# Strassen block products for four of eleven inner pairs of the second feed-forward matrix

## The chip, the cores and the metric

The kernel runs on one core of a Trainium2 chip. The metric is device time in microseconds (us), lower is better. One launch computes the whole two-layer trunk.

## The reference

A trunk of DEPTH = 2 layers over x of 256 tokens by 1024 channels, everything float32. Each layer has two feed-forward steps with a mixer between them. The change touches the feed-forward steps alone:

```python
def _swiglu(x, w1, w3, w2):
    return (jax.nn.silu(x @ w1) * (x @ w3)) @ w2
...
for l in range(DEPTH):
    h = _swiglu(x, ffn_w1[l, 0], ffn_w3[l, 0], ffn_w2[l, 0])
    x = _layernorm(ALPHA * x + 0.5 * h, ln_g[l, 0], ln_b[l, 0])
    h = _mixer(x, ...)
    x = _layernorm(ALPHA * x + h, ln_g[l, 1], ln_b[l, 1])
    h = _swiglu(x, ffn_w1[l, 1], ffn_w3[l, 1], ffn_w2[l, 1])
    x = _layernorm(ALPHA * x + 0.5 * h, ln_g[l, 2], ln_b[l, 2])
```

w1 and w3 are 1024 x 2816, w2 is 2816 x 1024. So there are four feed-forward steps in a launch, each with one product h @ w2 of 256 x 2816 by 2816 x 1024.

## The kernel before

**Precision.** A float32 operand is cut in two parts of a shorter format (F32R): `hi` is a ScalarE copy of the value, `lo` is a VectorE subtraction of `hi` from it. A product is then three matmuls, hi*hi, hi*lo and lo*hi (`three`, L205 to L208), all added up in one PSUM bank. A weight therefore needs one ScalarE and one VectorE instruction for each 128 x 1024 piece before the TensorE can read it.

**Streaming.** `stream` (L147) loads one chunk of 128 x 2048 float32 (1 MB) into a raw buffer, of which there are RAW = 4, and cuts it in pieces of 128 x 1024 (L166 for hi, L168 for lo). The pieces go to two pools, each with HL = 8 buffers (L42, L59, L60). A buffer comes free when the last matmul that reads it is done.

**The first half of a feed-forward step.** `gemm_a2` (L210) computes w1 and w3 products for two k tiles of h at a time, with h transposed, channels on the partitions: 32 matmuls of 512 columns with hi weights (L220) and 32 of 256 columns with lo weights (L227), then emptying of the banks (L228, L230), the silu, the multiplication (L524) and the split of h into `hh` and `hl` (L525, L174). It does so nine times. The first four k tiles of h come by another way (`gemm_first` or `gemm_b2`, and transposes).

**The second half, which the change rewrites.** h has 22 k tiles of 128 channels (FT = 22); w2 has two column halves of 512. `gemm_b` (L249) is called once for each half (L529, L536). In it, each k tile and each of the two token tiles of 128 costs one block product of 128 x 128 by 128 x 512, so three matmuls of 512 columns. The last `tail` k tiles are held, and done first for token tile 0, then for token tile 1, so that the norm of token tile 0 starts while token tile 1 is still on the TensorE. In the last feed-forward step of the launch, token tile 1 of the second half is computed as two blocks of 256 columns (`last`), so that only a quarter row is left for the end.

**The norm.** `Norm.part` (L412) adds a finished block to the scaled residual and takes statistics (L415, L419, in the last step also a multiplication, L421); `Norm.finish` (L423) normalizes a token tile; its transposes are put between later matmuls by counting beats.

**Order.** The TensorE's instructions run in the order in which the program writes them. The other engines' order is planned at build time: a scheduler takes, for each engine, the ready instruction of the lowest priority number, and the number grows by 1000 with each chunk (`step`, L105). On the chip each engine then runs its own list in order. PSUM has eight banks, four called main and four called side.

Of the kernel before, what the change touches and what calls it, by code (L numbers as in the profile page):

```python
# [11 lines left out]
F32 = mybir.dt.float32  # L12
F32R = mybir.dt.float32r
# [6 lines left out]
P = 128  # L20
# [5 lines left out]
DFF = 2816  # L26
FT = DFF // P
FB = 4
HEADS = 8
HD = 64  # L30
GROUPS = 8
# [16 lines left out]


@with_exitstack  # L50
def trunk(ctx, tc, x, xT, w13a, w13b, w2, wb, wqk, wa, wbr, wo, gateb, sgug, sgub, sguwT, sgubias, lam, diffg,
          lng, lnb, lngT, lnbT, cosT, sinT, out):
    nc = tc.nc
    V, A, G, PE = nc.vector, nc.scalar, nc.gpsimd, nc.tensor
# [15 lines left out]
    def name(s):  # L70
        serial[0] += 1
        return f"{s}_{serial[0]}"
# [11 lines left out]
    def view(tiles, per=2):  # L84
        return lambda k: tiles[k // per][:, (k % per) * T : (k % per + 1) * T]
# [57 lines left out]
    def behind(ins):  # L143

        return tc.issue_after(ins) if ins is not None else nullcontext()
# [93 lines left out]
    def rows_b(ps, t, k0, piece, xh, xl, kts, c0=0, n=512):  # L239
# [6 lines left out]
                  k == 0, k == kts - 1)  # L246
        beat(n / 1024)

    def gemm_b(src, kts, xh, xl, done, tail=4, last=()):  # L249

        blocks = [[(bank(), c, n) for c, n in (last if t else ()) or ((0, 512),)] for t in range(NT)]
        held = []
        for c in range(0, kts, 4):
            nk = min(4, kts - c)
            for i, piece in enumerate(stream(src[:, c * 512 : (c + nk) * 512], nk * 512)):
                k = c + 2 * i
                if k >= kts - tail:
                    held.append((k, piece))
                    continue
                for t in range(NT):  # L260
                    for ps, o, n in blocks[t]:
                        rows_b(ps, t, k, piece, xh, xl, kts, o, n)
        for t in range(NT):
            for ps, o, n in blocks[t]:
                for k, piece in held:
                    rows_b(ps, t, k, piece, xh, xl, kts, o, n)
                done(t, ps[:, :n], o, n)

    def gemm_b2(srcs, xh, xl, done, norm=None):

# [115 lines left out]
    class Norm:  # L386
# [25 lines left out]
        def part(self, t, c, ps):  # L412
            s = slice(c, c + ps.shape[1])
            with behind(self.xlo.get((0, 0))):
                V.scalar_tensor_tensor(out=self.y[t][:, s], in0=self.y[t][:, s], scalar=self.scale, in1=ps,  # L415
                                       op0=ALU.mult, op1=ALU.add)
            for o in range(s.start, s.stop, self.group):
                g = o // self.group * 6
                V.bn_stats(out=self.st[t][:, g : g + 6], in_=self.y[t][:, o : o + self.group])  # L419
            if self.last and t == NT - 1 and s.stop < D:  # L420
                V.tensor_tensor(out=self.y[t][:, s], in0=self.y[t][:, s], in1=self.g[:, s], op=ALU.mult)  # L421
# [70 lines left out]

    def ffn(l, f, i, norm, last=False):
        xh, xl = parts(both)
        h_hi = [act.tile([P, 512], F32R, tag="slot", name=name("hhi")) for _ in range(FT // 2)]
        h_lo = [act.tile([P, 512], F32R, tag="slot", name=name("hlo")) for _ in range(FT // 2)]
        hh, hl = view(h_hi), view(h_lo)

        def front(t, ps):
            s = t512("silu")  # L500
            A.activation(s, ps[0], AF.Silu)
            V.tensor_tensor(out=s, in0=s, in1=ps[1], op=ALU.mult)
            beside(turned(t, s), 2)

        def turned(t, s):
            b = side_bank()
            for k in range(FB):
                PE.transpose(b[:, k * P : (k + 1) * P], s[:, k * P : (k + 1) * P], ident)  # L508
            b4 = b.rearrange("p (k t) -> p k t", k=4)
            for j in range(2):  # L510
                hi = h_hi[j].rearrange("p (k t) -> p k t", k=2)[:, :, t * P : (t + 1) * P]
                lo = h_lo[j].rearrange("p (k t) -> p k t", k=2)[:, :, t * P : (t + 1) * P]
                split(hi, lo, b4[:, 2 * j : 2 * j + 2])
            yield 0

        if norm is None:
            gemm_first([w13b[l, f, 0], w13b[l, f, 1]], front)
        else:
            gemm_b2([w13b[l, f, 0], w13b[l, f, 1]], xh, xl, front, norm=norm)
        for j in range(FB, FT, 2):  # L520
            for m, z in gemm_a2([w13a[l, f, j - FB + m] for m in range(2)], both, lambda m: t512("silu")):
                s = z[:, :T]
                silu[0] = A.activation(s, s, AF.Silu).ins
                V.tensor_tensor(out=s, in0=s, in1=z[:, T:], op=ALU.mult)  # L524
# [6 lines left out]
        def done(t, p, c, n):  # L531
            ln.part(t, 512 + c, p)
            if c + n == 512:
                ln.finish(t, ((2, 1.5), (2, 1))[t])

        gemm_b(w2[l, f, 1], FT, hh, hl, done, tail=14, last=((0, 256), (256, 256)) if last else ())  # L536
        return ln.close()

    def mixer(l, i, norm):
# [222 lines left out]
    for l in range(DEPTH):  # L762
# [2 lines left out]
        norm = ffn(l, 1, 2, norm, last=l == DEPTH - 1)  # L765


_INS = ["x", "xT", "w13a", "w13b", "w2", "wb", "wqk", "wa", "wbr", "wo", "gateb", "sgug", "sgub", "sguwT", "sgubias",
        "lam", "diffg", "lng", "lnb", "lngT", "lnbT", "cosT", "sinT"]


def _layout(i):
    c = np.ascontiguousarray
    L = DEPTH
    f = {k: np.asarray(v) for k, v in i.items()}
    x = f["x"].reshape(T, D)
    o = {"x": x, "xT": c(x.reshape(T, KT, P).transpose(2, 1, 0)).reshape(P, KT * T)}

    def cols(w):

        k, n = w.shape[-2:]
# [24 lines left out]
    o["w13b"] = c(np.concatenate([halves(w1[..., :nb]), halves(w3[..., :nb])], axis=2))  # L806
    o["w2"] = halves(f["ffn_w2"])
# [40 lines left out]
```

## Time and profile before

| what | value |
|---|---|
| median of 3 runs | 1243.45 us (1243.18 to 1244.18) |
| span of the profiled execution | 1242.5 us, 0.95 us less than the median |
| TensorE matmul busy | 1236.6 us, 6703 instructions |
| VectorE busy | 873.1 us, 1532 instructions |
| ScalarE busy | 756.0 us, 1388 instructions |
| DMA | 241.87 MB, mean 195 GB/s |

The span is the time from the first to the last instruction of one profiled execution; the 0.95 us beside the median are what lies around it and the spread of runs. Busy time of an engine is the time in which at least one of its instructions ran. Matmuls overlap their neighbours, so what one costs is read from the distance of their starts, not from their length. In the rows "L208" is line 208 of the kernel, "bank<-whi,hhi" the output and the inputs by the program's names, "128x512" partitions by elements.

### The profile page before, as it was taken

How to read it: one execution, taken by the hardware profiler on the slowest of the kernel's cores; microseconds unless marked ns; L12 is line 12 of the kernel's file. 1: busy time of each engine (PE TensorE's matmuls, PEld its weight loads, DVE VectorE, ACT ScalarE, POOL GpSimd, SP SyncE). 2: the span in 40 equal slices, each digit the busy share in tenths (PEclk: the TensorE clock that was granted, in tenths of full speed). 3: DMA queues.
4: the chain of work that ended last, by engine and by line, in shares of the span. 5: the costliest groups of instructions: out<-in, count | busy, mean ns of one | idle time of the engine just before them, and what ended most of it. 6: DMA issues, size and time to landing. Idle time of an engine off the chain costs nothing.

```text
span 1242.5 us, 17870 instructions
## 1 busy us (share of the span) xinstructions
PE 1236.6 (100%) x6703; PEld 1064.1 (86%) x6703; DVE 873.1 (70%) x1532; ACT 756.0 (61%) x1388; POOL 86.0 (7%) x184
## 2 busy tenths in 40 slices
PE   9999999999999999999999999999999999999998
PEld 8888888888888888888888888888888888888887
DVE  6766567876587977665677665679756879766753
ACT  6776446679665566664466664466786555766640
POOL 0100000144100000000000000002430000000000
PEclk9999999999999999999999999999999999999999
DMA  9765645654754745556545546556556456455540
GB/s 352 276 204 183 224 171 187 227 167 165 248 183 145 244 162 205 177 180 253 194 169 191 192 159 250 203 184 206 162 175 228 165 174 233 170 203 203 165 174 35
DMA packets 40679, 241.87 MB, mean 195 GB/s; under 512 B 5344, under 2 KB 6416, under 8 KB 14480
## 3 DMA queue, kind: packets, MB, share of 16 engines
q1 hardware_dynamic: 36624, 227.82, 52.1%
q0 software_dynamic: 3536, 12.13, 3.0%
q8 instruction: 52, 0.85, 0.3%
q10 hardware_dynamic: 432, 0.79, 0.2%
q14 instruction: 35, 0.29, 0.1%
HBM read 235.47 MB, written 1.05 MB: 190 GB/s over the span
## 4 chain that ended last, share of the span: by engine, by line
PE 99%; DVE 0%; ACT 0%; issue 0%; DVEq 0%; ACTq 0%
PE bank L220 38%; PE bank L208 35%; PE bank L227 20%; PE bank L323 2%; PE sbank L588 1%; PE sbank L474 1%; PE sbank L637 1%; PE sbank L718 1%; PE sbank L335 0%; PE sbank L635 0%; PE sbank L659 0%; PE sbank L508 0%; PE sbank L622 0%; PE sbank L627 0%; PE sbank L446 0%; DVE xtok L454 0%
## 5 line engine op out<-in xcount | busy, mean ns | idle before, releaser
L168 DVE TENSOR_TENSOR wlo<-raw,whi 128x1024 fp32r<-128x1024 f32 (+1 forms) x442 | 490.0, 1127 | 223.4 <-PE bank L227 129.3
L166 ACT ACTIVATE whi<-raw 128x1024 fp32r<-128x1024 f32 (+1 forms) x442 | 425.8, 978 | 279.4 <-PE bank L208 135.3
L220 PE MATMUL bank<-x,whi 128*128 128x512 f32 x1792 | 426.5, 392 | 0.0
L220 PEld LDWEIGHTS bank<-x,whi 128*128 128x128 f32 x1792 | 330.7, 188 | 69.0 <-issue 2.6
L227 PE MATMUL bank<-x,wlo 128*128 128x256 f32 x1792 | 229.9, 284 | 0.0
L227 PEld LDWEIGHTS bank<-x,wlo 128*128 128x128 f32 x1792 | 224.2, 191 | 4.8
L208 PE MATMUL bank<-whi,hhi 128*128 128x512 f32 (+1 forms) x374 | 141.3, 378 | 0.0
L208 PE MATMUL bank<-wlo,hhi 128*128 128x512 f32 (+1 forms) x374 | 141.0, 377 | 0.0
L208 PE MATMUL bank<-whi,hlo 128*128 128x512 f32 (+1 forms) x374 | 140.9, 377 | 0.0
L228 ACT ACTIVATE r<-bank 128x256 f32<-128x256 f32 x256 | 96.5, 380 | 66.0 <-PE bank L227 65.7
L208 PE MATMUL bank<-whi,x 128*128 128x512 f32 x328 | 106.6, 394 | 0.0
L208 PEld LDWEIGHTS bank<-whi,hlo 128*128 128x128 f32 x374 | 70.4, 188 | 13.0
L208 PEld LDWEIGHTS bank<-wlo,hhi 128*128 128x128 f32 x374 | 70.4, 188 | 12.7
L208 PEld LDWEIGHTS bank<-whi,hhi 128*128 128x128 f32 x374 | 70.4, 188 | 12.7
L208 PEld LDWEIGHTS bank<-whi,x 128*128 128x128 f32 x328 | 61.6, 188 | 12.7
L208 PE MATMUL bank<-wlo,x 128*128 128x512 f32 x164 | 64.0, 390 | 0.0
L480 ACT ACTIVATE xf<-sbank,ln_b,ln_g 128x128 f32<-128x128 f32 x80 | 30.0, 456 | 40.2 <-PE sbank L474 40.2
L230 DVE TENSOR_TENSOR silu<-bank,r 128x256 f32<-128x256 f32 x144 | 54.2, 418 | 0.2
L383 POOL DMA_DIRECT2D bc<-in_lng x6 | 3.2, 530 | 727.7 <-DVE bc L382 727.7
L415 DVE SCALAR_TENSOR_TENSOR xtok<-xtok,bank 128x512 f32<-128x512 f32 (+1 forms) x25 | 16.6, 663 | 42.2 <-PE bank L208 42.2
L564 POOL TENSOR_TENSOR swap<-swap,sin_t 128x512 f32<-128x512 f32 x16 | 24.3, 1517 | 242.4 <-DMA swap<-z 226.7
L208 PE MATMUL bank<-lhi,x 128*128 128x512 f32 x120 | 39.9, 396 | 0.0
(183 smaller groups left out, 1254.1 us busy)
## 6 DMA issues: line engine op xcount, KB each, us to landing
raw<-in_w13a SPq DMA_DIRECT2D x72, 1024.0 KB, 5.0
raw<-in_w SPq DMA_DIRECT2D x40, 1024.0 KB, 4.9
raw<-in_wa SPq DMA_DIRECT2D x24, 1024.0 KB, 5.5
raw<-in_wb SPq DMA_DIRECT2D x16, 1024.0 KB, 4.9
raw<-in_wqk SPq DMA_DIRECT2D x16, 1024.0 KB, 5.1
raw<-in_wbr SPq DMA_DIRECT2D x16, 1024.0 KB, 4.9
raw<-in_w13b SPq DMA_DIRECT2D x12, 1024.0 KB, 5.0
raw<-in_wo SPq DMA_DIRECT2D x8, 1024.0 KB, 4.9
```

Source lines behind the costliest of these rows:

```text
L166: A.activation(h, r, AF.Copy)
L168: V.tensor_tensor(out=w, in0=r, in1=h.bitcast(F32), op=ALU.subtract)
L208: PE.matmul(ps, xx, w, start=start and n == 0, stop=stop and n == 2)
L220: PE.matmul(b[-1], hi[:, k * P : (k + 1) * P], xc(k), start=k == 0, stop=False)
L227: PE.matmul(b[n][:, :T], lo[:, k * P : (k + 1) * P], xc(k)[:, :T], start=False, stop=k == KT - 1)
L228: emptied[0] = A.activation(r[:, s], b[n][:, T:], AF.Copy, scale=scale).ins
L230: a = V.tensor_tensor(out=z[:, s], in0=b[n][:, :T], in1=r[:, s], op=ALU.add)
L323: PE.matmul(ps[t][m], x[:, j, o + t * P : o + (t + 1) * P], y, start=k0 + j == 0 and o == 0 and y is hi, stop=k0 + j == KT - 1 and y is lo)
L415: V.scalar_tensor_tensor(out=self.y[t][:, s], in0=self.y[t][:, s], scalar=self.scale, in1=ps, op0=ALU.mult, op1=ALU.add)
L474: PE.transpose(b[:, k * P : (k + 1) * P], self.y[t][:, h * 512 + k * P : h * 512 + (k + 1) * P], ident)
L480: A.activation(xf[:, s], b[:, s], AF.Identity, scale=self.gT[:, f], bias=self.bT[:, f])
L564: turned_by[0] = G.tensor_tensor(out=s3, in0=s3, in1=s, op=ALU.mult).ins
```

## The change

Of the eleven pairs of k tiles of h, four (k tiles 4 to 11) go through Strassen's scheme for 2 x 2 blocks: the two token tiles by the two k tiles of h, times the two k tiles by the two column halves of w2. Seven block products stand in place of eight. The other seven pairs stay as they were, and both column halves are now done together. The order on the TensorE is S, P, S, P, S, P, S (S a Strassen pair, P a plain pair), then the last four plain pairs, held, block by block: token tile 0 with both halves, then token tile 1 with both.

```diff
+NS = 4
+SQ = [(FB + 2 * p, FB + 2 * p + 1) for p in range(NS)]
+PQ = [(k, k + 1) for k in (0, 2, *range(FB + 2 * NS, FT, 2))]
...
-    act = ctx.enter_context(tc.tile_pool(name="act", bufs=27))
+    act = ctx.enter_context(tc.tile_pool(name="act", bufs=31))
...
+    def stream_s(src, pair):
...
+        a = (*pair, 0) if pair else None
+        if a is None:
+            pair = two()
+            a, keep = (*pair, 0), pair
+        else:
+            a, keep = (*pair, 512), None
+        b, c, d = ((*two(), 0) for _ in range(3))
+        cut(a, 0, 512)
+        cut(b, 1024, 1024)
+        V.tensor_tensor(out=raw[:, :1024], in0=raw[:, :1024], in1=raw[:, 512:1536], op=ALU.add)
+        cut(c, 0, 1024)
+        V.tensor_tensor(out=raw[:, 1024:1536], in0=raw[:, :512], in1=raw[:, 1024:1536], op=ALU.add)
+        V.tensor_tensor(out=raw[:, 1536:], in0=raw[:, 1024:1536], in1=raw[:, 1536:], op=ALU.add)
+        cut(d, 1024, 1024)
...
+        return keep, {1: at(a, 0), 3: at(b, 0), 2: at(b, 1), 5: at(c, 0), 7: at(c, 1), 6: at(d, 0), 4: at(d, 1)}
...
+        def mixed(q, qa):
+            qb = s512("qb")
...
+            for j, v in enumerate((qa, qb)):
+                split(at[0][j], at[1][j], v)
...
-                V.tensor_tensor(out=s, in0=s, in1=z[:, T:], op=ALU.mult)
-                split(hh(j + m), hl(j + m), s)
+                if (j, j + 1) in SQ:
+                    if m == 0:
+                        qa = s512("qa")
+                    V.tensor_tensor(out=qa[:, m * T : (m + 1) * T], in0=s, in1=z[:, T:], op=ALU.mult)
+                    if m:
+                        mixed((j, j + 1), qa)
...
-        gemm_b(w2[l, f, 0], FT, hh, hl, lambda t, p, c, n: ln.part(t, 0, p))
...
+        for n, q in enumerate(SQ):
+            pair, w = stream_s(w2s[l, f, n], pair)
+            for b in (3, 7, 4, 1, 2, 5, 6):
+                three(S[b], *s_op[q][b], *w[b], n == 0, n == NS - 1 and b in (1, 5, 6, 7))
+            beat(1.75)
+            if n < NS - 1:
+                plain_pair(False)
+        u, v = s512("u"), s512("v")
+        A.activation(u, S[6], AF.Copy)
+        ln.more(1, 0, S[7], ALU.subtract, ln.scale)
+        ln.more(0, 0, S[1], ALU.add, ln.scale)
+        V.tensor_tensor(out=u, in0=u, in1=S[1], op=ALU.add)
+        V.tensor_tensor(out=v, in0=S[5], in1=u, op=ALU.subtract)
+        ln.more(0, 1, v, ALU.add, ln.scale)
+        ln.more(1, 1, v, ALU.add, ln.scale)
+        ln.more(1, 0, u, ALU.add)
+        ln.more(1, 1, S[7], ALU.add)
+        while plain:
+            plain_pair(True)
+        for t in range(NT):
+            for c in range(2):
+                for ps, o, n in ends[t, c]:
+                    for q, w in held:
+                        rows_p(ps, t, q, w[c], hh, hl, o, n, stop=q == held[-1][0])
+                    for o in ((0, 256) if last and (t, c) == (1, 1) else (0,)):
+                        ln.part(t, c * 512 + o, ps[:, o : o + 256] if o or last and (t, c) == (1, 1) else ps, 1.0)
+            ln.finish(t, ((2, 1.5), (2, 1))[t])
...
-    nc = bacc.Bacc("TRN2", target_bir_lowering=False, num_devices=1)
+    nc = bacc.Bacc("TRN2", target_bir_lowering=False, num_devices=1, dynamic_dma_scratch_size=8192)
```

`stream_s` makes the seven weight operands of a pair: it cuts one 512-wide and three 1024-wide pieces and forms the sums between them in place, in the raw buffer. `two` takes one hi and one lo buffer; the 512-wide first piece shares its buffer between two successive Strassen pairs. `cut` is one ScalarE copy and one VectorE subtraction. `mixed` forms the sums of the h blocks with three VectorE instructions and splits 2 x 512 columns where two splits of 256 stood. Seven PSUM banks hold the products S1 to S7; four banks are the output blocks, of which three are S2, S3 and S4 themselves, so all eight banks are in use. `ln.more` is one VectorE instruction of 512 columns on the residual. The host packs w2 anew, in the same 1 MB chunks (eleven for each step, as many bytes as before).

More of the change, by code (lines that the diff above doesn't have):

```diff
@@ L247, in rows_b, with rows_p @@
         beat(n / 1024)
+    def rows_p(ps, t, q, piece, xh, xl, c0=0, n=512, stop=False, start=False):
+        for j, k in enumerate(q):
+            wh, wl = (v[:, j * 512 + c0 : j * 512 + c0 + n] for v in piece)
+            three(ps[:, :n], xh(k)[:, t * P : (t + 1) * P], xl(k)[:, t * P : (t + 1) * P], wh, wl,
+                  start and j == 0, stop and j == 1)
+        beat(n / 1024)
     def gemm_b(src, kts, xh, xl, done, tail=4, last=()):
@@ L267, in gemm_b, with two, cut, at @@
                 done(t, ps[:, :n], o, n)
+    def stream_s(src, pair):
+        step()
+        raw = raw_pool.tile([P, CH], F32, tag="raw", name=name("raw"))
+        nc.sync.dma_start(raw, src)
+        def two():
+            return hi_pool.tile([P, HC], F32R, tag="hi", name=name("shi")), lo_pool.tile([P, HC], F32R, tag="lo", name=name("slo"))
+        def cut(p, o, n):
+            h, w = (v[:, p[2] : p[2] + n] for v in p[:2])
+            r = raw[:, o : o + n]
+            with behind(latest[0]):
+                A.activation(h, r, AF.Copy)
+            with behind(latest[1]):
+                V.tensor_tensor(out=w, in0=r, in1=h.bitcast(F32), op=ALU.subtract)
+        a = (*pair, 0) if pair else None
[12 more added lines that the diff above has]
+        cut(d, 1024, 1024)
+        def at(p, j):
+            return tuple(v[:, p[2] + j * 512 : p[2] + j * 512 + 512] for v in p[:2])
+        return keep, {1: at(a, 0), 3: at(b, 0), 2: at(b, 1), 5: at(c, 0), 7: at(c, 1), 6: at(d, 0), 4: at(d, 1)}
     def gemm_b2(srcs, xh, xl, done, norm=None):
@@ L494, in ffn @@
         xh, xl = parts(both)
-        h_hi = [act.tile([P, 512], F32R, tag="slot", name=name("hhi")) for _ in range(FT // 2)]
-        h_lo = [act.tile([P, 512], F32R, tag="slot", name=name("hlo")) for _ in range(FT // 2)]
-        hh, hl = view(h_hi), view(h_lo)
+        h_hi, h_lo = ({q: act.tile([P, 512], F32R, tag="slot", name=name(n)) for q in PQ} for n in ("hhi", "hlo"))
+        f_hi, f_lo = ([d[k, k + 1] for k in range(0, FB, 2)] for d in (h_hi, h_lo))
+        h_hi, h_lo = ({k: d[q][:, j * T : (j + 1) * T] for q in PQ for j, k in enumerate(q)} for d in (h_hi, h_lo))
+        hh, hl = h_hi.get, h_lo.get
+        s_op = {}
+        def mixed(q, qa):
+            qb = s512("qb")
+            a = qa.rearrange("p (k t) -> p k t", k=4)
+            V.tensor_tensor(out=qb[:, :T].rearrange("p (k t) -> p k t", k=2),
+                            in0=a[:, 1:2].to_broadcast([P, 2, P]), in1=a[:, ::3], op=ALU.subtract)
+            V.tensor_tensor(out=qb[:, T : T + P], in0=qb[:, P:T], in1=qa[:, :P], op=ALU.subtract)
+            V.tensor_tensor(out=qb[:, T + P :], in0=qa[:, T : T + P], in1=qb[:, T : T + P], op=ALU.add)
+            if q == SQ[-1]:
+                at = [[v[:, j] for j in range(2)] for v in (act.tile([P, 2, 512], F32R, tag="val", name=name("sv"), bufs=2)
+                                                            for _ in range(2))]
+            else:
+                at = [[act.tile([P, 512], F32R, tag="slot", name=name(n)) for _ in range(2)] for n in ("shh", "shl")]
+            for j, v in enumerate((qa, qb)):
+                split(at[0][j], at[1][j], v)
+            s_op[q] = {n: tuple(at[o][j][:, c * P : (c + 1) * P] for o in range(2))
+                       for n, j, c in ((1, 0, 0), (2, 0, 2), (4, 0, 3), (7, 1, 0), (5, 1, 1), (6, 1, 2), (3, 1, 3))}
         def front(t, ps):
@@ L528, in ffn @@
         ln = Norm(l, i, 2.0 * ALPHA, 4.0 * EPS, s[:, :1], last)
-        gemm_b(w2[l, f, 0], FT, hh, hl, lambda t, p, c, n: ln.part(t, 0, p))
[L531 to L536, printed above, removed]
+        S = {n: side_bank() for n in (3, 7, 4)}
+        S.update({n: bank() for n in (1, 2, 5, 6)})
+        ends = {(0, 0): [(S[2], 0, 512)], (0, 1): [(S[3], 0, 512)], (1, 0): [(S[4], 0, 512)],
+                (1, 1): [(side_bank(), 0, 512)]}
@@ new lines, in ffn, with plain_pair @@
+        pair, held, plain = None, [], list(PQ)
+        def plain_pair(hold):
+            q = plain.pop(0)
+            w = stream(w2p[l, f, PQ.index(q)])
+            if hold:
+                held.append((q, w))
+                return
+            for c in range(2):
+                for t in range(NT):
+                    for ps, o, m in ends[t, c]:
+                        rows_p(ps, t, q, w[c], hh, hl, o, m, start=q == PQ[0] and t + c == 2)
+        for n, q in enumerate(SQ):
[5 more added lines that the diff above has]
+                plain_pair(False)
@@ L537, in ffn @@
+        for t in range(NT):
+            for c in range(2):
+                for ps, o, n in ends[t, c]:
[4 more added lines that the diff above has]
+            ln.finish(t, ((2, 1.5), (2, 1))[t])
         return ln.close()
@@ L806, in _layout, with blocks @@
     o["w13b"] = c(np.concatenate([halves(w1[..., :nb]), halves(w3[..., :nb])], axis=2))
-    o["w2"] = halves(f["ffn_w2"])
+    w2 = f["ffn_w2"].reshape(L, 2, FT, P, 2, 512)
+    def blocks(at):
+        return c(np.stack([w2[:, :, k, :, h] for k, h in at], axis=3)).reshape(L, 2, P, CH)
+    o["w2s"] = c(np.stack([blocks(((a, 0), (a, 1), (b, 1), (b, 0))) for a, b in SQ], axis=2))
+    o["w2p"] = c(np.stack([blocks(((a, 0), (b, 0), (a, 1), (b, 1))) for a, b in PQ], axis=2))
     u, v, q, k, val, ga, gb = (f["w_in"][:, :, s * D : (s + 1) * D] for s in range(7))
```

25 lines of the change are left out of this document (18 added, 7 removed).

## The prediction, made before the changed kernel ran

> **What bounds the kernel now.** I read the busy shares and the chain of work that ended last first: they say whether any engine but one matters.
>
> ```profile
> span 1242.5 us, 17870 instructions
> PE 1236.6 (100%) x6703; PEld 1064.1 (86%) x6703; DVE 873.1 (70%) x1532; ACT 756.0 (61%) x1388; POOL 86.0 (7%) x184
> PE 99%; DVE 0%; ACT 0%; issue 0%; DVEq 0%; ACTq 0%
> ```
>
> The TensorE (PE) is 99% of the chain. So a matmul taken out is time won, and VectorE (DVE) or ScalarE (ACT) work that is added is free until it keeps a matmul waiting. What one matmul is worth I take from the chain in order of time (start, length, what), which merges unbroken runs; it covers the end of the first half of step 1, its second matrix, and the last step.
>
> ```profile
> 117.62 7.28 PE bank L220 x32
> 124.90 3.83 PE bank L227 x32
> 128.73 57.15 PE bank L208 x252
> ...
> 1174.14 60.83 PE bank L208 x330
> ```
>
> 252 matmuls of 512 columns in 57.15 us are 0.2268 us each, with no gap. Then the engines by stretch: two pairs of the first half (the earlier one with POOL's loads of constants), and the second matrix with the norm behind it (columns: stretch, length, busy and count of PE, PEld, DVE, ACT, POOL, clock, DMA share, GB/s).
>
> ```profile
> 39.81:50.92 11.11, 11.11 (x66) 9.85 (x65) 8.27 (x22) 7.85 (x14) 4.96 (x9) 1.00 0.89 313
> ...
> 106.47:117.58 11.11, 11.11 (x66) 9.84 (x65) 7.29 (x13) 7.06 (x12) 0.00 (x0) 1.00 0.56 191
> 128.73:200.00 71.27, 71.27 (x324) 58.86 (x323) 44.40 (x74) 31.64 (x49) 1.06 (x2) 1.00 0.57 208
> ```
>
> DVE has a third of its time free in the last two, ACT more; the granted clock is 1.00.
>
> **What goes.** Each Strassen pair has 7 x 3 = 21 matmuls for 24. Four pairs in four steps save 48. Steps 1 to 3 go from 264 to 252 matmuls each: 12 x 0.2268 = 2.72 us, three times 8.16 us. The last step has 330 now, since one of its blocks is done in 256-wide halves, and these start 0.12 us apart:
>
> ```profile
> 1228.56 0.28 PE L208 MATMUL bank<-whi,hlo 128*128 128x256 f32 x1
> 1228.68 0.28 PE L208 MATMUL bank<-whi,hhi 128*128 128x256 f32 x1
> ```
>
> Two of those cost 0.24 for the 0.227 of a wide one. The change makes this block wide, so the step becomes 252 x 0.2268 = 57.15: 60.83 - 57.15 = 3.68 us less. Together **-11.84 us**.
>
> A Strassen product changes the PSUM bank after three matmuls, where L208 does it after six. The start of the kernel has the threes already (two hi, one lo, then the next bank):
>
> ```profile
> 25.60 0.62 PE L323 MATMUL bank<-whi,x 128*128 128x512 f32 x2
> 26.05 0.39 PE L323 MATMUL bank<-wlo,x 128*128 128x512 f32 x1
> 26.28 0.62 PE L323 MATMUL bank<-whi,x 128*128 128x512 f32 x2
> ```
>
> From 25.60 to 26.28 are 0.68 us for three, 0.227 each: changing banks costs nothing.
>
> The Trainium skill ("TensorE: Matmul & The Clock Gate", Back-to-back issue gap) speaks against this price: it gives about 131 ns for a 512-column matmul in a real stream, by which 48 of them would be only 6.3 us. The trace has 226.8 ns in the very stage, close to the 216 ns which the same section gives for the isolated gap, so the trace decides.
>
> **What comes: DVE and ACT beside the matmuls.** The prices, from the groups (mean ns of one) and from DVE's order in time:
>
> ```profile
> L168 DVE TENSOR_TENSOR wlo<-raw,whi 128x1024 fp32r<-128x1024 f32 x360 | 436.7, 1227 | 213.1 <-PE bank L227 126.8 <-ACT whi L166 70.7 <-issue 15.2
> L166 ACT ACTIVATE whi<-raw 128x1024 fp32r<-128x1024 f32 x360 | 378.2, 1059 | 225.8 <-PE bank L220 125.8 <-PE bank L208 91.5 <-ACT hhi L173 3.1
> L465 DVE TENSOR_TENSOR xtok<-xtok,bc 128x1024 f32<-128x1024 f32 x20 | 24.1, 1220 | 0.0
> L415 DVE SCALAR_TENSOR_TENSOR xtok<-xtok,bank 128x512 f32<-128x512 f32 x23 | 15.7, 684 | 39.1 <-PE bank L208 39.1
> L548 ACT ACTIVATE val<-bank 128x512 f32<-128x512 f32 x8 | 4.5, 592 | 1.1 <-PE bank L208 1.1
> ```
> ```profile
> 121.65 0.42 DVE L174 TENSOR_TENSOR hlo<-silu,hhi 128x256 fp32r<-128x256 f32 x1
> 125.89 1.22 DVE L168 TENSOR_TENSOR wlo<-raw,whi 128x1024 fp32r<-128x1024 f32 x1 [3.81 <-PE bank L227]
> 127.03 0.75 DVE L230 TENSOR_TENSOR silu<-bank,r 128x256 f32<-128x256 f32 x2
> 127.69 1.22 DVE L168 TENSOR_TENSOR wlo<-raw,whi 128x1024 fp32r<-128x1024 f32 x1
> 128.83 0.42 DVE L524 TENSOR_TENSOR silu<-silu 128x256 f32<-128x256 f32 x1
> 129.16 0.75 DVE L230 TENSOR_TENSOR silu<-bank,r 128x256 f32<-128x256 f32 x2
> ...
> 132.09 2.36 DVE L168 TENSOR_TENSOR wlo<-raw,whi 128x1024 fp32r<-128x1024 f32 x2
> ...
> 159.59 0.68 DVE L415 SCALAR_TENSOR_TENSOR xtok<-xtok,bank 128x512 f32<-128x512 f32 x1
> 160.19 1.22 DVE L168 TENSOR_TENSOR wlo<-raw,whi 128x1024 fp32r<-128x1024 f32 x1
> 161.32 0.69 DVE L419 BATCH_NORM_STATS2 st<-xtok 128x6 f32<-128x512 f32 x1
> ...
> 183.78 3.70 DVE L168 TENSOR_TENSOR wlo<-raw,whi 128x512 fp32r<-128x512 f32 x6
> ```
>
> In a row DVE takes 2.36 - 1.22 = 1.14 us for 1024 columns, (3.70 - 0.69) / 5 = 0.60 for 512, 0.33 for 256 (L230: 0.75 - 0.42). The in-place sums of `stream_s` are not in the trace; their nearest row, L465, in place and 1024 wide, costs what L168 does, so I take the same rate.
>
> *First half.* A Strassen pair adds three sums of h blocks (0.33 and two of about 0.2) and splits 2 x 512 for 2 x 256 (1.20 for 0.67): +1.3 us of DVE, in four pairs of 11.11 us. 7.29 becomes 8.6. What hides it is the 3.81 us in which DVE waits for a lo buffer that PE has yet to free; with that gone it would cost at most the 1.3 us by 16 pairs, 21 us. The sums of h are needed only in the second half, 50 us later. I take 0.
>
> *Second half.* One Strassen chunk costs DVE four lo parts (0.60 + 3 x 1.14) and three sums (1.14 + 2 x 0.60): 6.4 us; a plain one 2 x 1.14 = 2.3. For S and P together DVE needs 8.6 us, ACT (at most 3.5 + 2 copies of 1.06) 5.8, and PE gives 21 x 0.2268 + 24 x 0.2268 = 4.76 + 5.44 = **10.2 us**. So DVE is at 85%, with 1.6 us to spare in each turn: the bound has not changed, but it is near. The chunks stay 1 MB, 2 MB in 10.2 us, with four raw buffers and this time to landing (last column, us):
>
> ```profile
> raw<-in_w SPq DMA_DIRECT2D x40, 1024.0 KB, 4.9
> ```
>
> *The handover to the held pairs* is the tight place. PE wants the first halves of all four held pairs within 18 matmuls: the lo part of the fourth is read 19 x 0.2268 = 4.3 us after the last Strassen matmul. The eight buffers hold just these four pairs; the last Strassen pair frees its own after 12, 15, 18 and 21 of its 21 matmuls, and the fourth pair's first half gets the third of them, 0.7 us before the end. ACT, busy with the third pair from 2.0 before, copies it from +0.1 to +1.2; DVE has its lo at about **+2.4 us**. That is in time by 1.9, if DVE takes it before the sums that follow the last product: the copy of S6 (0.59, L548) is not ready before +0.7, and then come six dependent sums of 0.68 (L415).
>
> *Moves that cost nothing by this trace.* Both halves' `part` now lie in the held block, 24 matmuls = 5.4 us apart, and token tile 0 is finished 48 matmuls (10.9 us) before the end, for 42 (9.5 us) now: the next matrix starts no later. POOL's smaller scratch space concerns loads issued by 50.9 us (the nine of the stretch from 39.81) and used by `more` some 32 us after 128.73; that cover is over 100 us. The `act` buffers of the held and the Strassen pairs (26 of 31, as 22 of 27 before) leave the same five free.
>
> *The very end.* Now it looks so:
>
> ```profile
> 1235.00 0.43 DVE xtok L415
> 1235.43 0.02 issue
> 1235.45 0.44 DVE st L419
> 1235.89 0.02 issue
> 1235.91 0.27 DVE mv L426
> ```
>
> After the change both quarters of the last block come at once, and the first has three operations (L415, L419, L421) that were hidden under 42 narrow matmuls. Three more of 0.33 to 0.43 on DVE: at least 0.5 (two overlapped by dependences), at most 1.3. I take +0.9.
>
> **Sum.** -11.84 + 0.9, and +0.5 for small waits in the four handovers (0 to 2 each is priced below): -10.4. Span 1242.5 becomes 1232.1; the median stands 0.95 above the span, so **1233.0 us**.
>
> **The rivals.**
>
> *A. The sums go ahead of the fourth held pair* in DVE's list. Then the lo part comes at 0.7 + 6 x 0.68 + 1.2 = 6.0 and PE waits 1.7 us, in four steps 6.8: about 1239.3. For it: the sums belong to an earlier chunk, so they have the lower priority number. Against: the planner fills gaps by readiness; at 160.19 it put a weight's lo between two dependent instructions of the norm, and at 127.69 between the emptying of banks.
>
> *B, slower. DVE works the Strassen chunk in written order.* Each chunk then waits twice for an ACT copy of 1.06 between a sum and the next lo part: 8.6 + 2.1 = 10.7 for a turn of 10.2, so the lead is eaten, and DVE ends the last Strassen chunk just when PE wants it. PE wants the piece `d` 1.4 us after the chunk's start and so reaches the held pairs 3.4 us later; it wants the seventh of their pieces at 3.4 + 4.3 = 7.7, while DVE needs 7 x 1.14 + 8 sums of 0.68 = 13.4. Lost: 5.7 and some 0.5 a turn, less about 1.5 of lead at the start, 5.7 a step, 23 in all: about 1255. It decides from 10.9 / 4 = 2.7 us of waiting in each step on. Against it again 127.69 and 160.19: what is not ready is passed over, and the second and third sum don't need the copy of `c`, so they can fill the wait. For it: the plan is made at build time, and with 85% on DVE a small error in it isn't made up. The Trainium skill ("VectorE: DVE Perf Modes", The DRAIN you can't avoid) adds to this side: the next operation doesn't start before the pipe is empty. By it a turn would cost full durations, 9.4 of 10.2 us. The rows at 132.09 show starts 1.14 apart for a length of 1.22, so the trace has a little overlap.
>
> *C. A product less is worth half its spacing,* because matmuls overlap (0.28 long, 0.12 apart at 1228.56): 48 x 0.113 = 5.4, about 1238. The unbroken 57.15 us for 252 speak against it.
>
> *D. The saved matmuls come back* by waits of another kind, as for a bank of the previous pair: about 1243. S1 to S6 in main banks are reached after 9 free matmuls (2.0 us), and the last bank of the first half is emptied at 129.16 + 0.75 = 129.91, 1.2 us after its end at 128.73.
>
> **Chances.** Forecast (1231 to 1237) 0.64; A 0.14; B 0.14; C 0.02; D 0.06. A measurement of this kernel tells about 0.2% (2.5 us) from no change, so faster means below 1241.0. Forecast, C and most of A (0.12) are faster: 0.78; D and 0.02 of A are the same: 0.08; B is slower: 0.14. The range reaches from 1231 (no wait, the end at +0.5, less than half a microsecond of spread) over A to 1241.5.
>
> **What would show it.** PE near 6703 - 48 - 66 = 6589 instructions, starts still 0.227 apart; the second matrix of each step 57.2 us unbroken in the chain; DVE busy about 100 us higher (four steps of 4 x 1.3 + 4 x 4.1 + 8 x 0.6), ACT about 30. A gap of PE at the first matmuls of the held block, ended by DVE's lo, would be A; gaps in the turns too would be B; a wait of PE for ACT or DVE in the first half would overturn the zero there.

## The result, and the profile after

The changed kernel takes **1231.36 us** (median of 4 runs, 1231.01 to 1231.67) for 1243.36 us before (4 runs, 1243.18 to 1244.18): a ratio of 0.9902, 95% interval 0.9888 to 0.9916. Forecast were 1233.0 us.

The page of the changed kernel, the same rows as before:

```profile
span 1229.5 us, 17890 instructions
PE 1223.3 (99%) x6589; PEld 1050.6 (85%) x6589; DVE 980.3 (80%) x1692; ACT 781.1 (64%) x1424; POOL 87.0 (7%) x184
PE 99%; DMA 0%; DVE 0%; ACT 0%; DVEq 0%; issue 0%; ACTq 0%
```

PE has 114 matmuls less, 48 + 66, and is still 99% of the chain; DVE has 107 us more (about 100 forecast), ACT 25 (30 forecast), and both are still at 0% of it. (In the changed kernel `three` is L211, the cuts of `stream_s` are L293 and L295, its in-place sums L306 to L309, and `stream`'s lo part is L171.)

The chain of the changed kernel in order of time (start, length, what), step 1 and then the last step:

```profile
128.55 2.07 PE sbank L211 x9
130.62 4.08 PE bank L211 x18
...
161.22 8.16 PE bank L211 x36
169.38 12.24 PE sbank L211 x54
181.62 0.44 PE sbank L532 x4
...
1164.46 2.07 PE sbank L211 x9
...
1205.28 16.34 PE sbank L211 x72
1221.62 0.02 issue
```

The pieces are cut only where the output passes from side banks (products 3, 7, 4) to main banks; each begins where the one ahead ends, in the rows left out too. In the last step 252 matmuls run from 1164.46 to 1221.62: 57.16 us, 0.2268 each, the bank changing every three. So the Strassen pairs cost PE exactly their count.

Where the 13.0 us between the two spans went, from the starts in the two chains (the medians differ by 12.0 only; the point on the offset of the median, further down, says why):

| stretch | before, us | after, us | difference |
|---|---|---|---|
| second matrix of step 1 to the start of the mixer's own matmuls | 71.34 | 68.60 | -2.74 |
| second matrix of step 2 to the first half of step 3 | 84.13 | 81.39 | -2.74 |
| as step 1, for step 3 | 71.35 | 68.60 | -2.75 |
| second matrix of the last step | 60.83 | 57.16 | -3.67 |
| a part of each mixer (projections and attention) | 120.29, 120.61 | 119.83, 119.85 | -1.22 |
| last matmul to DVE's last wide operation | 3.10 | 3.84 | +0.74 |
| from there to the end of the span | 4.43 | 4.04 | -0.39 |
| start-up, to the second matrix of step 1 | 128.73 | 128.55 | -0.18 |

What DVE had left beside the second matrix of step 1, in the stretches of the changed kernel (columns as in the prediction): the second turn of S and P, and the whole from the first Strassen matmul to the held pairs.

```profile
138.75:148.95 10.20, 10.20 (x47) 8.45 (x46) 10.10 (x12) 6.55 (x7) 0.00 (x0) 1.00 0.56 204
128.55:163.94 35.39, 35.39 (x158) 29.30 (x157) 31.59 (x39) 19.89 (x25) 1.06 (x2) 1.00 0.73 261
```

DVE is busy 89% of the Strassen turns, in one of them 99%, and PE doesn't wait.

### The profile page after: what moved, and what is told of

Same layout as the page of the kernel before. It is cut to its first block, busy times and chain, and to the rows that moved or that the text cites. A ratio compares the mean times of both kernels' runs of the same rounds, so it can differ in the third digit from the quotient of the medians.

```text
span 1229.5 us, 17890 instructions
## 1 busy us (share of the span) xinstructions
PE 1223.3 (99%) x6589; PEld 1050.6 (85%) x6589; DVE 980.3 (80%) x1692; ACT 781.1 (64%) x1424; POOL 87.0 (7%) x184
## 4 chain that ended last, share of the span: by engine, by line
PE 99%; DMA 0%; DVE 0%; ACT 0%; DVEq 0%; issue 0%; ACTq 0%
PE bank L223 38%; PE bank L211 23%; PE bank L230 20%; PE sbank L211 12%; PE bank L371 2%; PE sbank L707 1%; PE sbank L532 1%; PE sbank L756 1%; PE sbank L837 1%; DMA xraw<-in_xT 0%; PE sbank L754 0%; PE sbank L778 0%; PE sbank L585 0%; PE sbank L741 0%; PE sbank L746 0%; PE sbank L504 0%
## 5 line engine op out<-in xcount | busy, mean ns | idle before, releaser
L171 DVE TENSOR_TENSOR wlo<-raw,whi 128x1024 fp32r<-128x1024 f32 (+1 forms) x410 | 450.0, 1116 | 109.1 <-PE bank L230 62.9
L169 ACT ACTIVATE whi<-raw 128x1024 fp32r<-128x1024 f32 (+1 forms) x410 | 388.8, 970 | 186.9 <-PE bank L223 114.8
L211 PE MATMUL bank<-whi,x 128*128 128x512 f32 x328 | 106.6, 394 | 0.0
L293 ACT ACTIVATE shi<-raw 128x1024 fp32r<-128x1024 f32 (+1 forms) x64 | 60.4, 950 | 61.0 <-DVE raw L309 39.1
L295 DVE TENSOR_TENSOR slo<-raw,shi 128x1024 fp32r<-128x1024 f32 (+1 forms) x64 | 69.3, 1088 | 24.8 <-PE bank L230 15.3
L211 PEld LDWEIGHTS bank<-whi,x 128*128 128x128 f32 x328 | 61.6, 188 | 12.7
L211 PE MATMUL sbank<-whi,hhi 128*128 128x512 f32 x168 | 65.7, 391 | 0.0
L211 PE MATMUL sbank<-whi,hlo 128*128 128x512 f32 x168 | 65.4, 389 | 0.0
L211 PE MATMUL sbank<-wlo,hhi 128*128 128x512 f32 x168 | 65.4, 389 | 0.0
L211 PE MATMUL bank<-wlo,x 128*128 128x512 f32 x164 | 64.0, 390 | 0.0
L211 PE MATMUL bank<-lhi,x 128*128 128x512 f32 x120 | 39.2, 395 | 0.0
L211 PEld LDWEIGHTS sbank<-whi,hlo 128*128 128x128 f32 x168 | 31.5, 188 | 6.7
L211 PEld LDWEIGHTS sbank<-wlo,hhi 128*128 128x128 f32 x168 | 31.6, 188 | 6.5
```

The source lines that it names most:

```text
L169: A.activation(h, r, AF.Copy)
L171: V.tensor_tensor(out=w, in0=r, in1=h.bitcast(F32), op=ALU.subtract)
L211: PE.matmul(ps, xx, w, start=start and n == 0, stop=stop and n == 2)
L293: A.activation(h, r, AF.Copy)
L295: V.tensor_tensor(out=w, in0=r, in1=h.bitcast(F32), op=ALU.subtract)
```

## The experiments

All are edits of the changed kernel but the last one, under "The mixers", which edits the kernel before. Times are single runs, each beside a single run of the kernel before (1243.4 or 1243.6 us), but for the version with both, which has 4 runs.

### The matmul's price: the eighth product put back

```diff
                 three(S[b], *s_op[q][b], *w[b], n == 0, n == NS - 1 and b in (1, 5, 6, 7))
+                if b == 4:
+                    three(S[4], *s_op[q][4], *w[4], False, False)
```

> The changed kernel with an eighth block product (product 4 once more, three matmuls) in each Strassen pair, so that PE does as many 512-wide matmuls as before while DVE and ACT keep the added work. It adds the seventh product twice, so the output changes. Theory: a matmul is worth its spacing of 0.2268 us and the added DVE and ACT work is hidden: 48 x 0.2268 = 10.9 us more than the changed kernel's 1231.4, so 1242.3. Rival C (half a spacing): 1236.8. If the DVE work were partly exposed in the changed kernel, the longer turns would hide it and the loss would be smaller than 10.9.

Measured: 1242.07 us, span 1240.4 for 1229.5: 10.9 us more in the span, 10.7 in the time. Forty-eight matmuls are worth 48 spacings of 0.2268. Rival C falls, and so does any partly exposed DVE work, which longer turns would have hidden.

### Rival A forced: the sums ahead of the fourth held pair

First, how the changed kernel itself has DVE's list at the handover of step 1, from its timeline (start, length, engine, line, what; in brackets the idle time before and what ended it):

```profile
155.88 3.49 DVE L171 TENSOR_TENSOR wlo<-raw,whi 128x1024 fp32r<-128x1024 f32 x3
160.37 1.23 DVE L171 TENSOR_TENSOR wlo<-raw,whi 128x1024 fp32r<-128x1024 f32 x1 [0.99 <-ACT whi L169]
...
163.03 3.50 DVE L171 TENSOR_TENSOR wlo<-raw,whi 128x1024 fp32r<-128x1024 f32 x3 [0.24 <-ACT whi L169]
166.44 0.68 DVE L640 TENSOR_TENSOR u<-u,bank 128x512 f32<-128x512 f32 x1
```

The first matmul behind the Strassen products starts at 161.22 + 12 x 0.2268 = 163.94. The seventh weight part of the held pairs (three, one and the third of the next three) ends at 163.03 + 3.50 = 166.53, 2.6 us after it; the prediction had 2.4. It is needed at 163.94 + 4.3 = 168.2, so 1.7 us are to spare (1.9 in the prediction). The first of the six sums, `u`, comes behind it. Now the other order:

```diff
-        ln.more(1, 1, S[7], ALU.add)
+        summed = ln.more(1, 1, S[7], ALU.add)
...
-            w = stream(w2p[l, f, PQ.index(q)])
+            w = stream(w2p[l, f, PQ.index(q)], after=(summed, summed) if hold and not plain else (None, None))
```

> The changed kernel with the lo parts of the fourth held pair queued on DVE behind the last of the sums that follow the Strassen products: rival A of the prediction, forced. If the handover is as tight as worked out, PE waits some 1.7 us there in each of four steps: about 6.8 us more, 1238.2, with a gap of PE 18 to 19 matmuls into the held block that a lo part ends. If the handover has more room than worked out, less than 2 us.

Measured: 1244.14 us, **12.8 us more** (span 1242.4, 12.9 more), twice what was expected, all of the gain gone. PE's own waits in this kernel, its matmuls behind the first of them, and ScalarE's copy ahead of the sums (step 1):

```profile
PE bank L211 <- DVE wlo L171: 10.9, 4, 2.8
```
```profile
170.33 0.50 PE L211 MATMUL bank<-wlo,hhi 128*128 128x512 f32 x1 [2.84 <-DVE wlo L171]
...
171.66 0.63 PE L211 MATMUL bank<-whi,hlo 128*128 128x512 f32 x1
172.08 0.63 PE L211 MATMUL sbank<-whi,hhi 128*128 128x512 f32 x1
```
```profile
161.18 2.96 ACT L169 ACTIVATE whi<-raw 128x1024 fp32r<-128x1024 f32 x3 [1.60 <-PE bank L211]
164.04 0.57 ACT L636 ACTIVATE u<-bank 128x512 f32<-128x512 f32 x1
```

The place is the one expected, the second matmul of the fourth held pair, and a lo part ends the wait. Its size is 2.84, 2.84, 2.84 and 2.36 us for 1.7. Two things make the difference in step 1, where the second matrix begins at 127.80 and the Strassen products end at 163.19. The copy of S6 is done at 164.61, 1.4 us after them and not 0.7, since ACT has three weight copies ahead of it; and DVE puts a weight part of the next matrix (0.6 us) ahead of the last sum.

Two costs come on top of the waits. In steps 2 and 3, at a granted clock of 1.00, the way from the first Strassen matmul to that of the next step is 3.1 us longer than in the changed kernel (184.95 for 181.81, 430.21 for 427.09): a wait costs some 0.3 us more than its length. And in step 1 the matmuls behind it soon start 0.42 apart (171.66 and 172.08), where 0.227 is normal: the granted clock fell, which cost about 1.6 us (the last section has its rows). So 10.9 us of waits, four times 0.3 beside them and 1.6 of clock, less the 0.75 by which step 1's second matrix began sooner than in the changed kernel, are the 12.9.

### Rival B forced: DVE in written order

Each lo part and each in-place sum of the second matrix is queued behind the one written ahead of it:

```diff
+    chain = [None]
...
-            with behind(latest[1]):
-                V.tensor_tensor(out=w, in0=r, in1=h.bitcast(F32), op=ALU.subtract)
+            with behind(chain[0] or latest[1]):
+                chain[0] = V.tensor_tensor(out=w, in0=r, in1=h.bitcast(F32), op=ALU.subtract).ins
```

(and the same around the three sums and the plain pairs' lo parts).

> The changed kernel with DVE's lo parts and in-place sums of the second matrix chained in the order in which the program writes them, over all Strassen and plain chunks of the step: rival B of the prediction, forced. By its working the turns take 10.7 us of DVE for 10.2 of PE and the held pairs come late: about 23 us more, 1254. If the lead that DVE has before the turns and at the handover is larger than worked out, less: under 8 us would say that the order of DVE's list hardly mattered.

Measured: 1269.83 us, 38.5 more than the changed kernel, for 23 expected. PE's waits in it:

```profile
PE bank L215 <- DVE wlo L173: 16.2, 7, 3.5
PE sbank L215 <- DVE slo L299: 6.6, 9, 0.8
PE sbank L215 <- ACT shi L297: 0.4, 1, 0.4
```

They add up to 23.2 us, as the working had it: 0.8 us at the third and fourth Strassen chunk in most steps, 3.46 at the held pairs in every step, with 0.6 to 1.0 more behind it in three. Of the other 15 us, 11 are clock, which the working left out: a mean of 0.991 over a span of 1268.1 us is 11 us lost, and the clock fell behind every gap of 3.46. The last 4 are about what 17 waits cost beyond their length, at the 0.3 us seen with the sums first (an estimate). So rival B was a real mechanism, and what kept it away is the planned order, in which DVE passes over what is not ready.

### How much room DVE has: one or three more operations in each chunk

```diff
+        for _ in range(1):
+            V.tensor_tensor(out=raw[:, :1024], in0=raw[:, :1024], in1=raw[:, :1024], op=ALU.max)
         cut(d, 1024, 1024)
```

> The changed kernel with one more in-place DVE operation of 1024 columns (1.14 us) in each Strassen chunk, which leaves its values as they are. By the prediction's sum a turn of S and P then takes 9.8 us of DVE for 10.2 of PE: still hidden, 1231 to 1232. If the time that DVE has to spare in a turn is used up (the stretch from 138.75 shows it busy 10.10 of 10.20 us), then about 1 us a turn comes out as a wait at the handover: 2 to 3 us a step, 1240 to 1243.

Measured: 1231.69 us: nothing (0.3 us, within the spread of runs). In its stretch from the first Strassen matmul to the held pairs of step 1:

```profile
128.50:163.90 35.40, 35.40 (x158) 29.30 (x157) 35.17 (x43) 19.45 (x26) 1.06 (x2) 1.00 0.68 245
```

DVE is busy 99.4% of it, and PE 100%. With `range(3)`:

> The same with three more such operations in each Strassen chunk: 12.0 us of DVE a turn for 10.2 of PE. Both readings expect a loss here: by the prediction's sum 1.8 us for each of three turns less the lead, with the handover behind it, some 4 to 6 us a step, 1247 to 1256. A time below 1235 would say that DVE is not the next bound at all.

Measured: 1284.84 us, 53.5 more than the changed kernel, for 16 to 25 expected. PE's waits in it:

```profile
PE bank L211 <- DVE wlo L171: 24.6, 11, 3.6
PE sbank L211 <- DVE slo L295: 8.0, 8, 1.9
PE sbank L211 <- ACT shi L293: 2.6, 1, 2.6
```

These are 35 us, and the mean clock of 0.989 is another 14. Twenty waits at some 0.3 us beyond their length would more than cover the remaining 4 (an estimate). The edge is sharp: between 9.8 and 12.0 us of DVE in a turn of 10.2 lie 53 us.

### More Strassen pairs

Five pairs with three held (`NS = 5`, a plain pair only while more than three are left):

> The changed kernel with five Strassen pairs of eleven, in the order S P S P S P S S and three held pairs. Twelve matmuls less in the launch than the changed kernel's: 2.7 us, so 1228.6, if DVE keeps up: five S and three P are 38.7 us of DVE for 40.1 of PE. Against it: the last two Strassen pairs stand side by side, 6.4 us of DVE for 4.8 of PE, just ahead of the handover, and three held pairs leave 36 matmuls (8.2 us) behind the norm of token tile 0, for 48. If that is too much, waits at the last Strassen pair and 1231 to 1236.

Measured: 1239.57 us, 8.2 more than the changed kernel. PE waits for no weight part of the second matrix, but for the norm of token tile 0 and for ACT behind it:

```profile
PE sbank L533 <- DVE xtok L489: 4.1, 3, 2.4
PE bank L212 <- ACT x L177: 2.6, 3, 0.9
```

The chain in order of time at the end of step 1, in this kernel:

```profile
173.09 8.17 PE sbank L212 x36
181.27 0.02 issue
...
182.88 0.60 DVE llo L172
...
184.20 0.56 DVE xtok L489
...
184.80 0.67 PE sbank L533 x4
...
185.49 1.51 ACT xf L539 x4
...
187.71 3.29 PE bank L212 x12
```

The chain leaves PE at 181.27 for DVE's work on token tile 0. PE itself still has matmuls of token tile 1 until 183.97; then it waits 0.83 us for the norm (L489) and, six matmuls later, 0.88 for ACT's part of the transposed activations (L539, L177), until 187.71. DVE's way there is stretched by weight parts of the next matrix put between (L172). The changed kernel has no such stop: its transposes (L532 at 181.62 in the first fence of its chain) follow without one.

Step 1 takes 70.63 us from the first Strassen matmul to the mixer's own, for 68.60 in the changed kernel; step 2, to the first half of step 3, 83.42 for 81.39; step 3 72.19 for 68.60. With the 0.7 us that each should have saved, 2.7, 2.7 and 4.3 us are lost; the last step, with no next matrix, saves its 0.7. In step 3 the wait for the norm is 2.40 us, and the chain runs back from it without PE for 24 us, through the weight parts of the held pairs, the sums and the statistics: there DVE was late already at the handover, and it showed at the norm. Another 1.0 us is in the two mixers (120.28 and 120.41 us for 119.83 and 119.85).

Six pairs, three held:

> Six Strassen pairs, S P S P S S S S and three held: 24 matmuls less than the changed kernel's (5.4 us), but 43 us of DVE for 39.5 of PE before the held block. Theory (DVE is the next bound): waits of PE in the last three Strassen pairs, some 4 us a step, so no faster than the changed kernel, 1232 to 1245. If the lead is larger than worked out: 1226.

Measured: 1281.61 us, 50 more and far above the 1232 to 1245 expected. PE waits 14.5 us for `wlo`, 5.7 and 4.2 for the Strassen parts, and the mean clock of 0.979, which the working had left out, is another 27 us.

Five pairs with four held, in two orders:

> Five Strassen pairs again, but with four held pairs as in the changed kernel: order S P S P S S S. Theory: what cost time with three held pairs was the norm of token tile 0, which had 36 matmuls for cover and not 48, and not DVE's weight parts; then with four held pairs that wait is gone. DVE needs 36.4 us for 34.7 of PE before the held block, 1.7 us over, as with one more operation a chunk (36.9 for 35.4), which was hidden: about 1228.7. Rival: three Strassen pairs in a row leave DVE no plain chunk to fill with; waits at the last of them, over 1231.

> The same five Strassen and four held pairs, with the second plain pair one place later: S P S S P S S. Same sums; if only the total of DVE's work counts, the same time as with S P S P S S S within 0.5 us. If the place of the plain pair matters (their two buffers come free earlier or later), a different one.

Measured: 1258.45 and 1259.93 us. The norm's wait is gone, as expected, but the weights are late: the times are the rival's (over 1231) and not the theory's. PE's waits in the first:

```profile
PE bank L212 <- DVE wlo L172: 14.0, 5, 3.5
PE sbank L212 <- DVE slo L296: 4.4, 8, 0.9
```

DVE's total over the block was, by the working, about that of the kernel with one more operation; only there the excess is spread over plain chunks, and here it stands at the end, where the sums of the last products and the held pairs follow. So the total is not enough of a criterion; what fits all these runs is how late DVE is at the handover. That the place of the plain pair changes the time is not shown: of the 1.5 us between the two, 1.0 is there already at the first Strassen matmul of step 1 (128.82 for 127.83). It does move the waits, to 18.6 us for `wlo` and 0.8 for `slo`.

### The end, and a version with both

```diff
+        if last:
+            ln.more(1, 1, ends[1, 1][0][0], ALU.add)
+            ends[1, 1] = [(bank(), 0, 256), (bank(), 256, 256)]
         while plain:
```

(the first bank closes its accumulation at the last plain pair ahead of the held ones).

> The changed kernel (four pairs) with the last block of the launch in two 256-wide halves again: what the plain pairs have added to it before the held block is summed out by one DVE operation, and the held pairs go to two banks of their own. From the end of the last matmul to the start of DVE's last wide operation were 3.84 us in the changed kernel and 3.10 before. Theory: that comes back to about 3.1, for 24 matmuls as 48 narrow ones (0.3 us more): the end 0.4 us earlier. If the two statistics and the multiplication are not the reason, it stays at 3.8.

Measured: 1231.97 us in a single run, 0.6 above the changed kernel's median, with a span of 1229.4 for 1229.5: the time does not tell the two apart. The chain at its end, and under it that of the changed kernel (whose last matmul ends at 1221.62):

```profile
1222.21 0.02 issue
...
1225.32 0.75 DVE xtok L512
```
```profile
1221.65 0.75 DVE xtok L472 x2
1222.40 0.66 DVE st L477 x2
1223.06 0.33 DVE xtok L479
...
1225.46 0.75 DVE xtok L512
```

From the last matmul to the last wide operation are 3.11 us for 3.84: the three extra operations (L472, L477, L479) were the reason. Counted from the first Strassen matmul of the step it saves 0.4 us.

The last kernel adds to this five Strassen pairs in the last step alone, where no next matrix waits for the norm:

```diff
+        sq = SQL if last else SQ
+        pq = [q for q in PQ if q not in sq]
+        spare = 3 if last else 4
```

> The changed kernel with the split end of the run before and, in the last feed-forward step of the launch alone, five Strassen pairs (S P S P S P S S, three held), since no next matrix waits for its norm. Theory: three matmuls less there (0.7 us), no wait of PE from DVE's weight parts as with five pairs before, and 0.4 us at the end: 1.1 us less than the changed kernel, 1230.3, ratio to the kernel before 0.9895. If the last Strassen pairs side by side do make a wait in this step, 1231 to 1234. The difference from the changed kernel is below what the time can tell, so the chain of the last step decides.

Measured: **1230.18 us** (4 runs, 1229.59 to 1230.75), ratio to the kernel before 0.9893 (0.9876 to 0.9909). The intervals of the two ratios overlap, so by time it is not told from the changed kernel. In the chain of the last step, from the first Strassen matmul to DVE's last wide operation, it takes 1224.20 - 1164.13 = 60.07 us for 1225.46 - 1164.46 = 61.00: 0.9 us less, 1.1 expected. DVE is now in the chain of the last 12 us, with the norm of token tile 0 in it, which lies nearer to the end.

### The mixers

> The kernel before with the change's two pool sizes alone (31 act buffers for 27, 8192 bytes of scratch for 16384). The trace after is about 1.2 us shorter than the removed matmuls and the end explain: 0.46 us in the mixer of the first layer and 0.76 us in that of the second. Theory P: the four more act buffers made those waits shorter; then this kernel's span is about 1.2 us below 1242.5, and both mixers are as short as in the changed kernel. Rival Q: they come from how the runs or the plan of the rest happen to fall; then the span stays at 1242.5 and the mixers are as before.

Measured: 1243.7 us, span 1242.0, and the mixers take 120.29 and 120.66 us, as before. So the pool sizes are not the cause. Where it is, from the chain of the second mixer, before and after:

```profile
894.43 0.63 PE sbank L588 x2
895.06 0.13 issue
895.19 1.10 PE sbank L588 x6
```
```profile
885.49 1.06 PE sbank L707 x8
```

The same eight matmuls of the attention scores take 1.86 us before and 1.06 after: there is a gap between the second and the third of them before. The first mixer shows 1.52 for 1.06. In ScalarE's list of the kernel before, a gate's tanh stands at this place and waits 1.21 us for DVE; after, the same operation waits 0.33 (in the first mixer):

```profile
276.22 0.51 ACT L681 ACTIVATE gate<-gz,gbh 128x256 f32<-128x256 f32 x1 [1.21 <-DVE gz L230]
```
```profile
272.00 0.51 ACT L800 ACTIVATE gate<-gz,gbh 128x256 f32<-128x256 f32 x1 [0.33 <-DVE gz L233]
```

It does not go with the Strassen products as such. The forced order of rival A has both mixers at 119.83, and the eighth product 119.83 and 120.15, though their second matrices differ. The kernels with five or six Strassen pairs and three held ones in every step have 120.28 to 120.41, and in the first mixer of both this tanh waits 1.2 us, as before. That the planner's order of ScalarE is the cause is argued from these rows; it wasn't isolated in a kernel of its own.

## Why the prediction was right, point by point

- **What goes**, -11.84 us: measured -2.74, -2.74, -2.75 and -3.67, together -11.90. The price of 0.2268 was tested by itself (10.9 us for 48). The Trainium skill's figure of about 131 ns for a matmul in a stream ("TensorE: Matmul & The Clock Gate", Back-to-back issue gap) would have given 6.3 by estimate; the runs do not agree with it.
- **Banks changing after three matmuls**: no cost, 57.16 us for 252.
- **The first half**, taken as 0: PE doesn't wait there; it starts the second matrix at 128.55 for 128.73.
- **DVE beside the second matrix**, 85% of a turn, hidden: 89% over the Strassen block, hidden; and so is 99.4%. The bound was where it was put: with 12.0 us of DVE in a turn it costs 53 us. ACT's 5.8 us a turn should read 5.6 by its own terms; ACT was busy 6.55 in the turn shown, and PE did not wait for it there.
- **The handover**, +2.4 us for the fourth held pair against 4.3: 2.6 measured, and the weight parts did pass the six sums that depend on the last product. The +0.5 allowed for waits was not needed.
- **The very end**, +0.9: +0.74, and shown to be the three operations.
- **What was not in the sum**: 1.2 us in the mixers, which no term had, and 0.4 at the output. From DVE's last wide operation to the end are 4.04 to 4.13 us in every kernel with Strassen pairs, for 4.43 and 4.42 in the kernel before and in that with its pool sizes changed; the cause was not followed. Another 0.2 is at the start, where the runs differ by more than that (the second matrix of step 1 begins between 127.80 and 128.87). With them, and the 0.5 for waits not needed, the span fell by 13.0 and not 10.4.
- **The offset of the median** was too small. 0.95 us was the distance of one span from the median of several runs; where span and time belong to one execution, 1.7 us lie around the span (1231.23 and 1229.5; 1.7 to 1.9 in all runs here but one). By this the span of 1242.5 belongs to the slowest of the four runs before (1244.18). The forecast of the time does not hang on it, since the same 0.95 was taken off the median and put back; but it is why the spans differ by 13.0 and the medians by 12.0. The forecast of 1233.0 came out 1.6 too high; the 1.2 of the mixers and the 0.5 for waits are that much by themselves.
- **Rival A's price** was too low: 1.7 us a step was 2.84 in three of the four, since (as step 1 shows) the copy of S6 was ready at +1.4 and not +0.7 and a weight part of the next matrix slipped in as well; the price of a wait beyond its length and the half clock behind one of them came on top. Forced, it took the whole gain: it would have been a case of no change, and not of 4 us faster.
- **Rival B's price** of 23 us was right as a wait and left out the clock: 38.5 in all.

## What to carry to other kernels

In a kernel that is all matmul, an algorithm with fewer products pays its count times the spacing of starts, if the engines that prepare operands stay under the shorter turn; so write their sum for each turn first. Then look at the last handover, where several prepared operands are wanted at once: there 1.7 us of slack carried a gain of 12, and the order of one engine's list decided it. Going further (a fifth pair in every step) broke on the cover of the norm in one arrangement and on that handover in the other, not on the average load alone.

## What the runs showed of the hardware

A gap of PE can cost more than its length. Behind 2.84 us of idle PE the granted clock was 0.59 over the next 4.0 us in step 1, but 1.00 behind the same 2.84 in steps 2 and 3 and behind 2.36 in the last; behind 3.46 us (rival B) it was down in all four steps, in step 2 at 0.50 over 4.8 us:

```profile
170.30:174.30 4.00, 3.97 (x11) 3.14 (x12) 3.69 (x6) 0.00 (x0) 0.00 (x0) 0.59 0.47 123
602.00:606.00 4.00, 3.93 (x17) 3.27 (x18) 4.00 (x7) 0.00 (x0) 0.00 (x0) 1.00 0.43 119
```
```profile
612.20:617.00 4.80, 4.80 (x11) 3.84 (x12) 3.94 (x6) 0.00 (x0) 0.00 (x0) 0.50 0.92 355
```

The first fence is from the kernel with the sums first, the second from the one in written order (the seventh number is the clock). In the second, another wait of 0.78 us ends at 612.20, but the matmuls ahead of it already started 0.43 apart.

The length of one gap does not decide alone. With six pairs, in step 1, no wait before this fall is longer than 1.04 us:

```profile
159.66 0.50 PE L212 MATMUL sbank<-slo,shh 128*128 128x512 f32 x1 [0.76 <-DVE slo L296]
161.43 0.50 PE L212 MATMUL sbank<-shi,shh 128*128 128x512 f32 x1 [1.04 <-ACT shi L294]
162.69 0.79 PE L212 MATMUL sbank<-slo,shh 128*128 128x512 f32 x1 [0.76 <-DVE slo L296]
162.70:168.80 6.10, 6.10 (x14) 4.78 (x15) 4.73 (x5) 3.02 (x4) 0.00 (x0) 0.50 0.46 173
```

Three waits within 3.8 us, with three matmuls between them, were enough for 6.1 us at 0.50. The Trainium skill ("TensorE: Matmul & The Clock Gate", What's actually happening) gives a free-running window of about 3.4 us of idle time for the fall to half. The rows with 3.46 us agree; the fall behind 2.84 us, and the one behind three waits of at most 1.04, came without a gap of that length.
